# A rank scatter kernel: four groups in the Pool ring, twelve tiles as row copies, no drain flag, and a split last scatter

## The chip, the cores and the metric

The kernel runs on one core of one Trainium2 chip. The metric is device time in microseconds (us) of one execution; medians are of the runs of one kernel. The span of the profile is some 1.7 us shorter than the time, because it counts from the first to the last record of the core. Words used below: a *transfer* is one DMA that Pool issues, a load or a scatter; the *last landing* is the end of the last DMA packet; the *drain* is the instruction DRAIN of Pool near the end of a run, whose start and length are read from its record in the trace (no view of the profile lists it).

## The reference

```python
def reference(x, scores):          # x: 8 x 2048 x 2560 float32, scores: 8 x 2048
    order = np.argsort(scores, axis=1)
    ranks = np.argsort(order, axis=1)
    out = np.zeros_like(x)
    out[np.arange(8)[:, None], ranks, :] = x
    return out
```

Every row of 10 KB of `x` goes to the place in its batch that the rank of its score names: 168 MB read, 168 MB written, and no arithmetic on the rows.

## The kernel before

VectorE (DVE) counts the ranks. The rows move in two ways. A *bulk* tile is loaded into SBUF by GpSimd (Pool) as 128 partitions of two neighbouring rows (a group with two columns, 2560 KB) or one (a group with one column, 1280 KB), and written by one indirect scatter of 128 rows per column. A *row-copied* tile is written from DRAM to DRAM, one DMA of 10 KB for each row, issued by SP and Activation (ACT) in turn. The tiles of a group that are row-copied stand in the third place of `GROUPS`: all eight of the first column and three of the second, eleven tiles of 128 rows.

```python
GROUPS = [(0, 1, range(B)), (P, 1, range(3))] + [(256 * i, 2, ()) for i in range(1, 8)]
ORDER = [2, 0, 1, 3, 4, 5, 6, 7, 8]
SPLIT = ()          # groups whose scatters go out as the last 2 rows and the first 126
NBUF = 8            # SBUF buffers of the Pool ring
LAG = 2             # a load waits for the scatters of the group LAG places back
...
with tc.tile_critical(no_gpsimd_drain=True):
    ...
    # SP and ACT: 16 rows at a time, addresses read into registers
    for i in range(G):
        line.eng.dma_start(out=out_bytes[bass.ds(at[i], ROW)],
                           in_=x_bytes[b, row, :]).then_inc(s_rows[line], 16)
    ...
    for k in range(1, NBUF):
        load(pl, k, s_load[k])
    for k, (b, g) in enumerate(BULK):
        i = k % NBUF
        if k >= LAG and k + NBUF - LAG < len(BULK):
            scatters_done(pl, k - LAG)                  # Pool blocks here
            load(pl, k + NBUF - LAG, s_load[(k - LAG) % NBUF])
        ...                                             # wait for load k and its ranks
        for j in range(GROUPS[g][1]):
            scatter(k, j, 0, P, rank_i, s_scat[i][j])   # or the 2 and 126 rows of SPLIT
    for k in range(max(0, len(BULK) - NBUF), len(BULK)):
        scatters_done(sp, k)
```

## Time and profile before

| | before |
|---|---|
| time, median of 3 runs (lowest to highest) | 794.85 us (794.8 to 796.62) |
| span of the profiled execution | 795.4 us |
| DMA packets, bytes | 70737, 321.57 MB |
| last DMA packet ends | 790.9 us |
| Pool drain in the final barrier | 791.64 us, 3.0 us long |

The profile says that the sixteen DMA engines are busy nearly all the time, so the DMA engine that ends last is expected to set the time. Its main lines stand in the prediction below. Two more: how long a load takes from issue to landing (the issues of Pool: direction, engine, operation, count, size, median us), and SP's wait in the final barrier (total us, times, longest). The first says how much is queued ahead of a load; in the second SP waits 2.9 us after everything has landed, while Pool drains.

```profile
x<-in_x_dram POOLq DMA_DIRECT2D x55, 2560.0 KB, 19.2
out_dram<-x,rank_i POOLq DMA_INDIRECT x117, 23.5
```
```profile
SPq L420 <- PEq L420: 3.3, 2, 2.9
```

One caution belongs here. The profiled execution of before was a slowish one: it took 797.09 us.

### The profile page before, as it was taken

To read this page: it belongs to the slowest core of one execution; us is meant where nothing else is said; L and a number is where in the kernel's file an instruction comes from. 1 tells how busy PE (TensorE), PEld (TensorE's weight loads), DVE (VectorE), ACT (ScalarE), POOL (GpSimd) and SP (SyncE) were. 2 spreads that over 40 slices of the span, in tenths; PEclk is the share of its full clock that TensorE was granted. 3 is DMA by queue.
4 is the path that set the end of the run, shared out by engine and by line. 5 is a ranking of instruction groups with operands and counts; after the bars stand their busy time and mean duration, and the time that the engine had idled before them with its cause. 6 is when DMAs were issued, how large, how long until landed. Compare 5 with 4: busy or idle time off the path is not lost.

```text
span 795.4 us, 4586 instructions
## 1 busy us (share of the span) xinstructions
PE 33.3 (4%) x155; PEld 27.2 (3%) x155; DVE 411.2 (52%) x1002; POOL 148.4 (19%) x186
## 2 busy tenths in 40 slices
PE   3002010020020100200000000000000000000000
PEld 3001010010010100100000000000000000000000
DVE  6999999999999999999994000000000000000000
POOL 3102121212121212022111212122121212111600
PEclk9555555555555555555555555555555555555555
DMA  8999999999999999999999999999999999999994
GB/s 364 431 402 365 424 415 425 417 422 417 425 417 418 347 420 422 422 367 420 421 420 423 397 397 421 420 419 380 420 411 423 420 386 407 401 431 426 390 428 193
DMA packets 70737, 321.57 MB, mean 404 GB/s; under 512 B 25384, under 2 KB 47912, under 8 KB 47912
## 3 DMA queue, kind: packets, MB, share of 16 engines
q0 software_dynamic: 25488, 304.10, 91.3%
q1 hardware_dynamic: 22688, 9.94, 4.9%
q10 hardware_dynamic: 22528, 7.25, 3.9%
q14 instruction: 32, 0.26, 0.1%
q8 instruction: 1, 0.02, 0.0%
HBM read 167.84 MB, written 167.77 MB: 422 GB/s over the span
## 4 chain that ended last, share of the span: by engine, by line
DVE 47%; DMA 40%; issue 4%; POOL 3%; PE 1%; POOLq 0%; SPq 0%
DVE trash L258 41%; DMA out_dram<-x,rank_i 38%; DVE s_all L235 2%; DMA x<-in_x_dram 2%; POOL out_dram L361 2%; DVE rank L284 1%; DVE rank L290 1%; DVE rank_i L307 1%; POOL x L122 1%; DMA s_in<-in_scores_dram 0%; PE ps_all L190 0%; PE ps_col L169 0%; DVE rows_i L220 0%; POOLq L28 0%; DVE s_col L177 0%
## 5 line engine op out<-in xcount | busy, mean ns | idle before, releaser
L258 DVE TENSOR_SCALAR_CACHE_REDUCE trash<-s_all,s_col 128x1792 bf16<-128x1792 f32 (+9 forms) x248 | 315.3, 1306 | 0.3
L122 POOL DMA_DIRECT2D x<-in_x_dram x60 | 33.8, 565 | 545.8 <-DMA out_dram<-x,rank_i 376.5
L361 POOL DMA_INDIRECT out_dram<-x,rank_i x117 | 112.8, 964 | 59.0 <-issue 35.3
L258 DVE SCALAR_TENSOR_TENSOR trash<-s_all,s_col,mask 128x256 bf16<-128x256 f32 (+1 forms) x128 | 59.0, 461 | 0.0
L190 PE MATMUL ps_all<-ident,s_col 128*128 128x128 f32 x128 | 27.2, 399 | 247.4 <-DVE s_all L235 247.0
L190 PEld LDWEIGHTS ps_all<-ident,s_col 128*128 128x128 f32 x128 | 24.4, 213 | 249.4 <-DVE s_all L235 249.0
L235 DVE COPY s_all<-ps_all 128x512 f32<-128x512 f32 x32 | 20.1, 683 | 1.8 <-PE ps_all L190 1.5
L258 DVE DVE_READ_ACCUMULATOR trash<-s_all,s_col 128x1 f32 x248 | 19.9, 80 | 0.0
L290 DVE TENSOR_TENSOR rank<-rank,acc 128x2 f32<-128x2 f32 (+1 forms) x72 | 11.5, 160 | 2.5
L284 DVE TENSOR_TENSOR rank<-acc,acc 128x2 f32<-128x2 f32 (+1 forms) x72 | 11.5, 160 | 2.5
L307 DVE CAST rank_i<-rank 128x2 int32<-128x2 f32 (+1 forms) x61 | 10.7, 176 | 1.8
L258 DVE DVE_READ_ACCUMULATOR trash<-s_all,s_col,mask 128x1 f32 x128 | 10.2, 80 | 0.0
L300 PE MATMUL ps_row<-ident,rank 128*1 128x128 f32 x11 | 4.1, 372 | 101.3 <-DVE rank L290 92.7
L300 PEld LDWEIGHTS ps_row<-ident,rank 128*1 128x1 f32 x11 | 0.9, 79 | 105.0 <-DVE rank L290 95.5
L220 DVE TENSOR_SCALAR rows_i<-ps_row 1x128 int32<-1x128 f32 x11 | 3.0, 272 | 0.0
L177 DVE COPY s_col<-ps_col 128x128 f32<-128x128 f32 x1 | 0.3, 292 | 4.8 <-PE ps_col L169 4.8
L169 PE MATMUL ps_col<-ident,s_in 8*128 8x8 f32 x16 | 2.0, 261 | 4.0 <-DMA s_in<-in_scores_dram 4.0
L169 PEld LDWEIGHTS ps_col<-ident,s_in 8*128 8x128 f32 x16 | 1.9, 211 | 4.0 <-DMA s_in<-in_scores_dram 4.0
L150 POOL TENSOR_SCALAR_AFFINE_SELECT mask<-mask 128x256 f32<-128x256 f32 x2 | 0.8, 398 | 0.0
L162 DVE MEMSET acc<- 128x128 f32 x1 | 0.2, 165 | 1.1 <-SPq L98 1.1
L133 POOL MEMSET mask<- 128x512 f32 x1 | 0.5, 525 | 0.0
L132 POOL MEMSET ident<- 128x128 f32 x1 | 0.2, 204 | 0.5 <-SPq L98 0.5
(5 smaller groups left out, 0.7 us busy)
## 6 DMA issues: line engine op xcount, KB each, us to landing
x<-in_x_dram POOLq DMA_DIRECT2D x55, 2560.0 KB, 19.2
out_dram<-in_x_dram SPq DMA_DIRECT2D x704, 10.0 KB
out_dram<-in_x_dram ACTq DMA_DIRECT2D x704, 10.0 KB
x<-in_x_dram POOLq DMA_DIRECT2D x5, 1280.0 KB, 16.7
x<-in_x_dram SPq DMA_DIRECT2D x1, 2560.0 KB, 13.4
out_dram<-x,rank_i POOLq DMA_INDIRECT x117, 23.5
s_in<-in_scores_dram SPq DMA_DIRECT2D x1, 64.0 KB
```

What stands on the lines that cost most here:

```text
L122: line.eng.dma_start(out=xb[k % NBUF][:, :m * D], in_=x[b, r:r + P * m, :].rearrange("(p j) d -> p (j d)", j=m),).then_inc(sem, 16)
L150: nc.gpsimd.affine_select(out=part, in_=part, pattern=[[0, MMAX], [-1, P]], compare_op=OP.is_ge, fill=0.0, base=-half, channel_multiplier=1,)
L169: nc.tensor.transpose(out=ps_col[:, B * c:B * (c + 1)], in_=s_in[:, r + j:r + m * P:m], identity=ident[:B, :B],)
L190: nc.tensor.transpose(out=ps_all[:, P * c:P * (c + 1)], in_=s_col[:, c, b:b + 1].to_broadcast([P, P]), identity=ident[:],)
L220: nc.vector.tensor_scalar(out=rows_i[DIRECT.index((b, g))][:m, :], in0=ps_row[:m, :P], scalar1=float(b * N), scalar2=float(ROW), op0=OP.ad ...
L235: nc.vector.tensor_copy(out=s_all[:, 512 * q:512 * (q + 1)], in_=ps_all[:, 512 * q:512 * (q + 1)],)
L258: how.pop("do")(out=trash[i][:, :P * (hi_c - lo_c)], in0=s_all[:, P * lo_c:P * hi_c], accum_out=acc[which][:, col:col + 1], **how,)
L284: nc.vector.tensor_tensor(out=rank[:, cols], in0=acc[0][:, cols], in1=acc[1][:, cols], op=OP.add)
L290: nc.vector.tensor_tensor(out=rank[:, cols], in0=rank[:, cols], in1=acc[2][:, cols], op=OP.add)
L300: nc.tensor.transpose(out=ps_row[:m, :P], in_=rank[:, cols], identity=ident[:])
L307: nc.vector.tensor_copy(out=rank_i[:, cols], in_=rank[:, cols])
L361: nc.gpsimd.indirect_dma_start(out=out_flat, out_offset=bass.IndirectOffsetOnAxis(ap=index[:hi - lo, col:col + 1], axis=0), in_=xb[k % NBU ...
```

## The change

The intent: keep more groups queued, so that no DMA engine runs dry behind Pool's waits (LAG 2 to 4, no one-column groups, plain order); move one more tile from the bulk path to row copies (12 tiles: both columns of the first group, for six batches); let Pool drain before the closing block's last signals rather than in the final barrier; and split the last group's scatters in 2 and 126 rows, so that the sixteen engines end more evenly.

```diff
-    GROUPS = [(0, 1, range(B)), (P, 1, range(3))] + [(256 * i, 2, ()) for i in range(1, 8)]
-    ORDER = [2, 0, 1, 3, 4, 5, 6, 7, 8]
+    GROUPS = [(0, 2, range(6))] + [(256 * i, 2, ()) for i in range(1, 8)]
+    ORDER = range(8)
...
-    SPLIT = ()
+    SPLIT = [(7, 7)]
     LAST = 2
     NBUF = 8
-    LAG = 2
+    LAG = 4
...
-    with tc.tile_critical(no_gpsimd_drain=True):
+    with tc.tile_critical():
```

## The prediction

> **What bounds the kernel now.** I read the page's queue and busy rows first, then a table of windows, then Pool's waits and its timeline, and last the raw records behind them: each DMA packet's start and length, and the sixteen completion increments of each DMA.
>
> The page's busy row of the 16 DMA engines, and its queues (packets, MB, share of 16 engines):
>
> ```profile
> DMA  8999999999999999999999999999999999999994
> ...
> q0 software_dynamic: 25488, 304.10, 91.3%
> q1 hardware_dynamic: 22688, 9.94, 4.9%
> q10 hardware_dynamic: 22528, 7.25, 3.9%
> ```
>
> The shares add to 100.1%: the DMA engines are the bound. DVE ends at about 426 us and Pool is 19% busy; DVE is named on the first half of the chain of waits only because it happened to run beside Pool's waits. q0 carries loads and scatters, q1 and q10 the 1408 row copies.
>
> Full is not the same as useful. Windows of the same profile (PE, PEld, DVE, POOL busy, clock, DMA share, GB/s):
>
> ```profile
> 60.00:70.00 10.00, 3.67 (x16) 3.27 (x16) 9.79 (x22) 2.50 (x3) 0.64 1.07 359
> 260.00:270.00 10.00, 0.00 (x0) 0.00 (x0) 9.76 (x26) 2.49 (x3) 0.50 1.08 311
> 740.00:750.00 10.00, 0.00 (x0) 0.00 (x0) 0.00 (x0) 7.20 (x8) 0.50 0.99 381
> 760.00:770.00 10.00, 0.00 (x0) 0.00 (x0) 0.00 (x0) 0.00 (x0) 0.50 1.01 429
> ...
> 784.00:786.00 2.00, 0.00 (x0) 0.00 (x0) 0.00 (x0) 0.00 (x0) 0.50 0.14 56
> 786.00:788.00 2.00, 0.00 (x0) 0.00 (x0) 0.00 (x0) 0.00 (x0) 0.50 0.06 26
> ```
>
> 429 is full speed; 311 to 381 at a share near 1 means packets that wait inside (first packets of a load took 1.2 to 2.2 us in the records instead of 0.76). From 784 us the share is 0.06, one engine of sixteen: **a single DMA engine works on alone until 791**. The increments say the same of the whole run: in the last scatter 15 engines land within 1.1 us and one 6.1 us later, and from about 160 us on one lags by 5 to 9 us in nearly every transfer. I call it the slow engine. I could not read its number.
>
> Pool's waits (total us, times, longest), then one line of its timeline:
>
> ```profile
> POOL x L122 <- DMA out_dram<-x,rank_i: 376.5, 37, 31.5
> ```
> ```profile
> 63.73 0.57 POOL L122 DMA_DIRECT2D x<-in_x_dram  x1 [31.46 <-DMA out_dram<-x,rank_i]
> ```
>
> Before each load Pool waits for all sixteen increments of the scatters two groups back, that is for the slow engine. The others then hold one load and one group of scatters, about 12.5 us of work, less their lead of up to 9 us and about 4 us until a new load reaches them. Behind a one-column group it is half of that. So they run dry (263 to 272, 340, 440 to 480, 540, 640 to 690, 735 to 745 us); at each such place the lag shrinks by 1 to 5 us. The 63.73 line is the worst case: only the first two groups' scatters had been issued before Pool blocked, and just one was left when it woke.
>
> **What the Trainium skill says.** "DMA: Bandwidth & Descriptors", section "Queues, rings and completion order": an engine round-robins between its queue rows by packet. The trace agrees: on the slow engine row copies and q0 packets, completion packets included, go one to one (44 to 44 from 280 to 300 us). Same page, "Why a DMA increments its semaphore by 16 and not by 1": only the full 16 means landed, and the number of engines is the largest divisor up to 16 of the slowest dimension, with an exception for some GpSimd copies that puts ceil(n/16) partitions on each. So 126 rows would be 9 on each of 14 engines, or 8 on fifteen and 6 on the last; no run here shows which. Same page, "Latency and other measured facts": engines 7 and 15 are usually slower. The trace shows one slow engine, in phases with loads only (the lag grows from 7.0 to 8.8 us between 700 and 745 us, and stays at 7.2 in the scatters after 751).
>
> **The change, part by part.** What counts is the slow engine, which ends at 791 us; 4.4 us of ending follow it.
>
> Its account now, worked out from packet lengths in the records (0.381 us per 10 KB of q0, 0.757 per 20 KB, 0.034 for a row copy's share of 640 bytes with its completion): 440 x 0.757 + 976 x 0.381 + 1408 x 0.034 = 753, its 8 packets of the first load 6, some instruction fetches and the scores about 2, so 761. It starts at 2.1 us and its first packets are 2.3 us long: 765. 791 - 765 = 26 us are left to explain. Between the dry places its lag grows by some 2.6% of the time (4.7 to 8.9 us from 113 to 272; 4.5 to 7.1 from 360 to 440), over 735 us about 19: its own slowness, which nothing in the change removes. The remainder, some 7, is what it loses itself at the dry places. A second reading: the last increments of consecutive transfers are 6.2 to 6.8 us apart for a load, but 10.4 after the 63.73 line (69.9 to 80.3), 8.2 at 280, and 0.4 to 1 too long at six later places: 3.8 + 1.5 + 3.6 = 9. I take 8.
>
> - Four groups in the ring, and no one-column groups. Scatters of four groups go out before the first wait (their ranks are ready by an estimated 42 us, while eight loads fill the queue to 56), and in steady state three groups, 37 us, stay queued behind the one waited for. That is more than any lead I expect (19 plus a few). All dry places go. The 15 fast engines gain some 17 us, but this is not in the sum: they only wait longer at the end. For the slow engine: **-8**.
> - Twelve tiles. Per engine a bulk tile is 16 x 0.381 = 6.1 us, a row-copied one 128 x 0.034 = 4.4: **-1.7**. DVE changes by a 2048-wide pass for a 1920-wide and a 128-wide one; it is idle after 426 us anyway.
> - Order 0, 1, 2...: the first scatter's ranks come one group, about 6 us, later, behind queued loads: 0.
> - Row copies reaching the end: 1536 rows against 57 x 9 + 116 x 9 = 1557 q0 packets, some 20 of them before the first row. At one to one they last as long as q0 itself, where before they ended at 727 on the slow engine. I estimate 10 to 20 rows left over; alone in the dry places, rows took 0.3 us each, several beside each other: **+2**.
> - Split scatters: if the slow engine is one of two left out by 14 engines of 9 rows, it loses 14 packets, -5.3; if it is the last of ceil(126/16), 4 packets, -1.5; else 0 to +0.8. My mixture: **-1.5**. The two added issues (1.25 us) lie far ahead of the data.
> - Pool drain. In the trace a GpSimd drain of 3.0 us starts at 791.64, in the final barrier. With the flag gone a drain takes the place of a NOP that waits for the same signal of SP at 791.56. I expect the 3 us to move forward by 0.1 and SP's collecting to come after it: **+0.2**, not -3.
>
> Sum: -8 - 1.7 + 2 - 1.5 + 0.2 = -9, so 794.85 becomes **786**.
>
> **The rivals.** *All the fast engines' gain counts*: if the slowness moves from engine to engine with the dry places, a loose ring averages it, the time falls by 17 or more to about 775. For it: after 272 us several engines lag 6 to 7.5 us. Against: the same growth returns after every reset. *Nothing to gain*: if the slow engine never waits and merely looks slow at the dry places, only 1.7 us and the split remain: 791 to 795. For it: at 340 to 357 us its transfers are evenly spaced although the others ran dry. *The row copies become the end*: the slots are used up, and the SP and Activation queues run on after q0, 5 to 10 us; 792 to 798. For it is the count 1536 to 1537; against it that 10 KB packets at the end give rows twice as many turns per us as 20 KB loads. *A really early drain* (beginning when Pool has issued its last, hidden beside the transfers) would take 3 us off each of these.
>
> **Range and chances.** The sum's uncertain terms are the 8 (4 to 13), the split (-5 to +1), the rows (0 to 8) and the drain (-3 to +0.3); together some 6 us either way. Low 777: first rival in part, or a lucky split and an early drain. High 795: second or third rival. 2% faster is 779, at the low edge, which needs two lucky terms: 0.17. 2% slower is 811, which needs a new stall: 0.02.
>
> **What would show it.** Right: window rates of 410 to 425 GB/s with no dip between 60 and 75 us or later; fifteen engines done some 15 to 20 us before the end and a share of 0.06 for that long; Pool's load waits all on scatters four groups back, no rates below 380 before 745; row copies issued until about 750; the drain 3 us long after the last landing. Wrong: an even end (all engines within 3 us) would say that the slowness was made by the ring; dips that stay would say it was not the depth; a last landing on q1 or q10 would be the third rival; a tail of one engine below 10 us with an unchanged time would say the lag was a sum I misread.

## The result

| | before | after |
|---|---|---|
| time, median of 4 runs | 794.83 us | 801.3 us (801.17 to 801.36) |
| ratio | | 1.0076, 95% interval 1.0059 to 1.0094 |
| span of the profiled execution | 795.4 us | 799.6 us |
| DMA packets, bytes | 70737, 321.57 MB | 74355, 320.29 MB |
| last q0 packet, last row copy end | 790.9, 726.8 us | 790.9, 790.9 us |
| Pool drain: start, length | 791.64, 3.0 us | 791.78, 7.0 us |

A ratio here and below is the mean time of one kernel's fast runs over that of the other's of the same rounds, so it is not quite the ratio of the medians quoted beside it. The change made the kernel slower by 6.5 us, outside the predicted range of 777 to 795 us.

The page's busy row of the DMA engines and its queues, after:

```profile
DMA  8999999999999999999999999999999999999930
...
q0 software_dynamic: 25008, 301.48, 88.8%
q1 hardware_dynamic: 24736, 10.60, 4.9%
q10 hardware_dynamic: 24576, 7.91, 4.0%
```

The last two slices now read 3 and 0 where before only the last was short, with a 4: the engines as a group end earlier. q0 (Pool's transfers) carries 480 packets fewer and q1 and q10 (the row copies) 4096 more, which goes with a twelfth row-copied tile, 32 packets for each of its 128 rows.

Windows after (columns as in the prediction: PE, PEld, DVE, POOL busy, clock, DMA share, GB/s):

```profile
60.00:70.00 10.00, 3.72 (x17) 3.29 (x17) 9.89 (x15) 2.49 (x3) 0.67 1.02 413
260.00:270.00 10.00, 0.20 (x1) 0.20 (x2) 9.72 (x27) 2.48 (x3) 0.50 1.04 431
740.00:750.00 10.00, 0.00 (x0) 0.00 (x0) 0.00 (x0) 1.90 (x2) 0.50 1.03 417
750.00:760.00 10.00, 0.00 (x0) 0.00 (x0) 0.00 (x0) 3.69 (x4) 0.50 0.96 359
760.00:770.00 10.00, 0.00 (x0) 0.00 (x0) 0.00 (x0) 0.00 (x0) 0.50 0.65 229
770.00:780.00 10.00, 0.00 (x0) 0.00 (x0) 0.00 (x0) 0.00 (x0) 0.50 0.08 28
780.00:790.00 10.00, 0.00 (x0) 0.00 (x0) 0.00 (x0) 0.00 (x0) 0.50 0.06 25
```

The three places that moved 359, 311 and 381 GB/s before now move 413, 431 and 417: these dips are gone, and from 60 to 750 us no window of 10 us is below 410. Two low ones are left: 374 GB/s from 50 to 60 us (381 before), and a new one of 359 from 750 to 760 us, where Pool waits for the last load before it issues the last scatters. From 770 us on the share is 0.06 to 0.08, one engine of sixteen. It works alone for some 20 us (from 771), where it had 6 before, and it ends at the same 790.9.

Pool's waits for its loads, the line of its timeline that answers to the one in the prediction, and its issues:

```profile
POOL x L122 <- DMA out_dram<-x,rank_i: 343.7, 33, 19.0
```
```profile
63.23 0.57 POOL L122 DMA_DIRECT2D x<-in_x_dram  x1 [18.99 <-DMA out_dram<-x,rank_i]
```
```profile
x<-in_x_dram POOLq DMA_DIRECT2D x57, 2560.0 KB, 46.5
...
out_dram<-x,rank_i POOLq DMA_INDIRECT x116, 51.1
```

The first wait fell from 31.5 to 19.0 us because four groups of scatters go out ahead of it. A load now lands 46.5 us after its issue instead of 19.2: that much is queued ahead. Pool still waits for 344 us, but from 60 to 750 us the rates show no sign that the DMA engines run dry behind it.

SP's wait at the end, after:

```profile
SPq L98 <- POOLq L98: 6.8, 1, 6.8
```

SP now waits on Pool at line 98, the closing of the block, as the missing flag makes it, and 6.8 us instead of 2.9.

**Where the 6.5 us come from.** Spans of typical executions, before (from b1, the kernel before without the flag, so with the same DMA program) against after: last landing 788.7 and 790.9 (+2.2); from there to the start of Pool's drain 0.6 and 0.9 (+0.3); the drain 3.0 and 7.0 (+4.0); the rest 0.8 and 0.8. The sum is +6.5, against spans of 793.2 and 799.6 (+6.4); the +2.2 is little more than what equal programs differ by (below), the +4.0 is clear. So there are two questions: why did the transfers not end 8 us earlier, and why is the drain longer?

### The profile page after: what moved, and what is told of

It is laid out like the page before. It is cut to its first block, busy times and chain, and to the rows that moved or that the text cites. A ratio compares the mean times of both kernels' runs of the same rounds, so it can differ in the third digit from the quotient of the medians.

```text
span 799.6 us, 4803 instructions
## 1 busy us (share of the span) xinstructions
PE 33.3 (4%) x152; PEld 28.7 (4%) x152; DVE 409.0 (51%) x963; POOL 147.6 (18%) x184
## 2 busy tenths in 40 slices
DMA packets 74355, 320.29 MB, mean 401 GB/s; under 512 B 27464, under 2 KB 52040, under 8 KB 52040
## 4 chain that ended last, share of the span: by engine, by line
DVE 45%; another core or an unknown queue 31%; POOL 8%; DMA 6%; issue 4%; PE 1%; POOLq 0%; SPq 0%
DVE trash L258 39%; POOL out_dram L361 6%; DMA x<-in_x_dram 6%; DVE s_all L235 2%; POOL x L122 2%; DVE rank L284 1%; DVE rank L290 1%; DVE rank_i L307 1%; PE ps_all L190 0%; DMA s_in<-in_scores_dram 0%; PE ps_col L169 0%; DVE rows_i L220 0%; POOLq L28 0%; DVE s_col L177 0%
## 5 line engine op out<-in xcount | busy, mean ns | idle before, releaser
L258 DVE TENSOR_SCALAR_CACHE_REDUCE trash<-s_all,s_col 128x1792 bf16<-128x1792 f32 (+7 forms) x240 | 314.4, 1344 | 0.3
L122 POOL DMA_DIRECT2D x<-in_x_dram x57 | 32.1, 563 | 510.4 <-DMA out_dram<-x,rank_i 343.7
L258 DVE SCALAR_TENSOR_TENSOR trash<-s_all,s_col,mask 128x256 bf16<-128x256 f32 x128 | 61.3, 479 | 0.0
L190 PE MATMUL ps_all<-ident,s_col 128*128 128x128 f32 x128 | 29.1, 421 | 275.1 <-DVE s_all L235 274.7
L190 PEld LDWEIGHTS ps_all<-ident,s_col 128*128 128x128 f32 x128 | 26.1, 227 | 277.0 <-DVE s_all L235 276.6
L290 DVE TENSOR_TENSOR rank<-rank,acc 128x2 f32<-128x2 f32 x64 | 10.3, 162 | 2.2
L284 DVE TENSOR_TENSOR rank<-acc,acc 128x2 f32<-128x2 f32 x64 | 10.3, 161 | 2.2
L307 DVE CAST rank_i<-rank 128x2 int32<-128x2 f32 x58 | 9.9, 171 | 1.8
L361 POOL DMA_INDIRECT out_dram<-x,rank_t x2 | 1.7, 872 | 11.6 <-DMA x<-in_x_dram 11.3
L300 PE MATMUL ps_row<-ident,rank 128*2 128x128 f32 x6 | 1.9, 322 | 13.3 <-DVE rank L290 13.3
L300 PEld LDWEIGHTS ps_row<-ident,rank 128*2 128x2 f32 x6 | 0.5, 80 | 15.6 <-DVE rank L290 15.6
## 6 DMA issues: line engine op xcount, KB each, us to landing
x<-in_x_dram POOLq DMA_DIRECT2D x57, 2560.0 KB, 46.5
```

The source lines that it names most:

```text
L122: line.eng.dma_start(out=xb[k % NBUF][:, :m * D], in_=x[b, r:r + P * m, :].rearrange("(p j) d -> p (j d)", j=m),).then_inc(sem, 16)
L190: nc.tensor.transpose(out=ps_all[:, P * c:P * (c + 1)], in_=s_col[:, c, b:b + 1].to_broadcast([P, P]), identity=ident[:],)
L258: how.pop("do")(out=trash[i][:, :P * (hi_c - lo_c)], in0=s_all[:, P * lo_c:P * hi_c], accum_out=acc[which][:, col:col + 1], **how,)
L284: nc.vector.tensor_tensor(out=rank[:, cols], in0=acc[0][:, cols], in1=acc[1][:, cols], op=OP.add)
L290: nc.vector.tensor_tensor(out=rank[:, cols], in0=rank[:, cols], in1=acc[2][:, cols], op=OP.add)
L300: nc.tensor.transpose(out=ps_row[:m, :P], in_=rank[:, cols], identity=ident[:])
```

## The experiments

My theory after the result: one DMA engine is slow by itself and has its own sum of work, so the ring gives it nothing; the split puts 9 packets on it and costs time; the drain is longer for a reason to be found. Rivals: the ring does help and something else takes the gain away (the split, the row copies at the end); the drain is long because of the missing flag, or because row copies are still in flight, or because of the number of Pool's transfers. Eighteen kernels were run, all with correct results, each against runs of the kernel before on the same chip (median 794.75 to 795.63 us). Last landings of kernels with the same DMA program differ by about 1 to 2 us (790.9 and 788.7; 790.9 and 789.7), so a landing alone settles nothing below that.

| run | time, us | ratio (95%) | last landing | Pool drain, us | Pool transfers |
|---|---|---|---|---|---|
| a1_flag_back | 800.23 | 1.0070 (1.0056-1.0083) | 789.7 | 7.010 | 175 |
| a2_two_groups | 801.14 | 1.0077 (1.0064-1.0091) | 791.6 | 7.010 | 175 |
| a3_no_split | 798.88 | 1.0051 (1.0037-1.0064) | 788.0 | 6.847 | 173 |
| b1_drain_alone | 795.12 | 1.0007 (0.9993-1.0020) | 788.7 | 3.011 | 177 |
| b2_four_groups | 793.69 | 0.9985 (0.9971-0.9999) | 787.4 | 3.178 | 177 |
| b3_twelve_tiles | 798.50 | 1.0047 (1.0034-1.0061) | 787.2 | 6.847 | 173 |
| c1_126_first | 802.80 | 1.0100 (1.0085-1.0116) | 791.7 | 7.010 | 175 |
| d1_ten_tiles | 797.48 | 1.0032 (1.0020-1.0045) | 787.2 | 7.092 | 176 |
| b4_split_alone | 799.61 | 1.0053 (1.0039-1.0067) | 793.4 | 3.178 | 179 |
| e1_rows_ten | 794.37 | 0.9986 (0.9972-1.0000) | 788.0 | 3.178 | 177 |
| e2_rows_five | 794.39 | 0.9985 (0.9972-0.9999) | 788.0 | 3.178 | 177 |
| e3_two_splits | 804.99 | 1.0118 (1.0103-1.0133) | 794.7 | 7.173 | 177 |
| g1_early_drain | 792.08 | 0.9956 (0.9936-0.9976) | 787.4 | 32.0, early | 177 |
| g2_extra_7_8_15 | 808.62 | 1.0161 (1.0138-1.0184) | 802.5 | 3.178 | 177 |
| g3_extra_4_10_12 | 803.52 | 1.0098 (1.0078-1.0118) | 797.4 | 3.178 | 177 |
| g4_one_column_kept | 799.70 | 1.0051 (1.0030-1.0071) | 787.9 | 8.725 | 175 |
| h1_low_engines | 818.15 | 1.0293 (1.0277-1.0309) | 813.5 | 32.1, early | 176 |
| h2_changed_early_drain | 796.54 | 1.0018 (1.0005-1.0032) | 789.9 | 40.1, early | 175 |

### Undoing one part of the change

**a1_flag_back**: the flag is put back.

```diff
-    with tc.tile_critical():
+    with tc.tile_critical(no_gpsimd_drain=True):
```

> The changed kernel with the Pool drain taken out of the end of the section again. Theory A (the drain is the whole loss): the last landing stays at 791 us, the drain in the final barrier is 3.0 us again, and the time falls from 801.3 to about 795 to 796, that is level with the kernel before within 0.3%. Rival B (the loss is in the transfers, or the longer drain belongs to the new scatters): the drain in the final barrier is 7 us and the time stays above 799.

800.23 us, with the drain back in the final barrier and as long as in the changed kernel, 7.010 us. The flag decides where the drain stands and not how long it is.

**a2_two_groups**: the ring of the changed kernel goes back to two groups.

```diff
-    LAG = 4
+    LAG = 2
```

> The changed kernel with two groups in the ring in place of four. Theory A (one DMA engine's own slowness sets the end; the ring only lets the others run ahead): the dips in GB/s and the resets of the lag come back, the slow engine's last landing stays within 1.5 us of 791, and the time is 800 to 803. Rival B (my prediction's step: the dry places cost the slow engine 8 us, and something else in the change took them back): the last landing moves to 797 or later and the time to 807 or more.

801.14 us, the same as the changed kernel. Its windows:

```profile
60.00:70.00 10.00, 4.05 (x17) 3.35 (x17) 9.89 (x15) 2.49 (x3) 0.50 1.09 362
...
770.00:780.00 10.00, 0.00 (x0) 0.00 (x0) 0.00 (x0) 0.00 (x0) 0.50 0.78 293
780.00:790.00 10.00, 0.00 (x0) 0.00 (x0) 0.00 (x0) 0.00 (x0) 0.50 0.13 39
```

The early dip is back (362 GB/s), and the fifteen fast engines work on until about 778 us, where most had ended by 767. The end has not moved. Ten microseconds of fifteen engines are worth nothing here.

**a3_no_split**: no split.

```diff
-    SPLIT = [(7, 7)]
+    SPLIT = ()
```

> The changed kernel with the last group scattered whole. The trace of the changed kernel shows 9 packets of 10 KB for the slow engine in each 126-row scatter, so Theory A (14 engines of 9 rows, the slow one among them): the last landing 0.8 to 1.2 us earlier, the time 800.2 to 800.6, the drain still near 7 us. Rival B (the split itself makes the drain long, as its scatters use 2 and 14 engines): the drain is back at 3 us and the time near 796.

798.88 us, so the split costs the changed kernel 2.4 us. Row copies end 0.2 us after the last scatter in this run, and 1.7 us pass from there to the drain instead of 0.9. Taking this part out leaves 4 us still lost.

**c1_126_first**: the 126 rows are issued ahead of the 2.

```diff
-                    scatter(k, j, P - LAST, P, rank_t, s_last[i][j])
                     scatter(k, j, 0, P - LAST, rank_i, s_scat[i][j])
+                    scatter(k, j, P - LAST, P, rank_t, s_last[i][j])
```

> The changed kernel with the 126-row scatter ahead of the 2-row one. If the engines for 126 rows are 14 consecutive ones from a cursor that stands at the first engine, they are now the first 14, and the 2 rows go to the last two. Theory A (the slow engine is one of the last two): it has 1 packet in place of 9 in each of the two scatters, 16 fewer at 0.415 us, so the last landing comes 6.6 us earlier, near 784, and the time is 794 to 795. Rival B (the slow engine is another, or there is no such cursor): within 1 us of the changed kernel, 800 to 802.

802.8 us: no relief. The packet records show 9 packets of 10 KB on the slow engine, alone by then, for each scatter of 126 rows, as in the changed kernel, where each holds it for some 3.8 us (783.1 to 787.0 and 787.2 to 790.9). If 126 rows go to 14 engines of 9 rows, the slow engine was not one of the two left out in either order.

**d1_ten_tiles**: ten tiles instead of twelve, and no split, so that the row copies end long before q0.

```diff
-    GROUPS = [(0, 2, range(6))] + ...
+    GROUPS = [(0, 2, range(5))] + ...
-    SPLIT = [(7, 7)]
+    SPLIT = ()
```

> The changed kernel without the split and with 10 tiles of row copies in place of 12, so that the row copies end well before the last scatters on the slow engine. Theory A (row copies run beside the drain's queue to the end and that is why the drain is long): the drain is near 3 us. Rival B (the drain counts Pool's own transfers, 176 here against 173 without the split): the drain stays at 6.8 to 7.1 us. By packet lengths two more bulk tiles cost the slow engine 3.4 us, so the last landing at 790 to 793.

797.48 us; the last row copy ends at 672 us and the drain still takes 7.092. So row copies near the end are not why it is long. The last landing is 787.2, against 788.0 of a3 with two tiles more and 787.4 to 788.0 of b2, e1 and e2 with one more: by packet lengths two tiles more in bulk should have cost 3.4 us. A row-copied tile is worth nothing that these runs can resolve.

### One part of the change alone

**b1_drain_alone**: the kernel before, without the flag.

```diff
-    with tc.tile_critical(no_gpsimd_drain=True):
+    with tc.tile_critical():
```

> The kernel before with the drain at the end of the section as the only edit. Theory A (where the drain stands decides its length): 7 us of drain after the last landing at 791, time 800 to 801. Rival B (the length comes from other parts of the change): a drain of 3 us and a time of 795 to 796.

795.12 against 794.9 us: +0.2, within the noise (interval 0.9993 to 1.0020), with a drain of 3.011 us that starts 0.6 us after the last landing.

**b2_four_groups**: the kernel before with four groups in the ring.

```diff
-    LAG = 2
+    LAG = 4
```

> The kernel before with four groups in the ring as the only edit. Theory A (the slow engine's own work sets the end, the ring gives nothing): the others end near 770 and the slow engine at 788 to 792, the drain is 3.0 us, time 794 to 796. Rival B (the ring does give the slow engine something when the row copies are not also made more): last landing at 783 or earlier, time below 789.

793.69 against 794.91 us, a gain of 1.2. Its windows:

```profile
60.00:70.00 10.00, 3.67 (x16) 3.27 (x16) 9.83 (x21) 2.50 (x3) 0.50 1.03 417
...
760.00:770.00 10.00, 0.00 (x0) 0.00 (x0) 0.00 (x0) 0.00 (x0) 0.50 0.63 262
770.00:780.00 10.00, 0.00 (x0) 0.00 (x0) 0.00 (x0) 0.00 (x0) 0.50 0.07 29
780.00:790.00 10.00, 0.00 (x0) 0.00 (x0) 0.00 (x0) 0.00 (x0) 0.50 0.05 19
```

Before, 359 GB/s from 60 to 70 us; here 417. Before, one engine was alone from about 785 us on; here from about 771 (most of the others end by 766). The ring does to the kernel before just what was predicted of it, and the end moves by 1.2 us. This is the plainest of the eighteen runs: the ring's effect on the fast engines and its lack of effect on the time, with nothing else changed.

**b3_twelve_tiles**: the kernel before with the new groups and order, eleven row-copied tiles becoming twelve and no one-column groups.

```diff
-    GROUPS = [(0, 1, range(B)), (P, 1, range(3))] + [(256 * i, 2, ()) for i in range(1, 8)]
-    ORDER = [2, 0, 1, 3, 4, 5, 6, 7, 8]
+    GROUPS = [(0, 2, range(6))] + [(256 * i, 2, ()) for i in range(1, 8)]
+    ORDER = range(8)
```

> The kernel before with the new groups and their order (12 tiles of row copies, no one-column groups) as the only edit: two groups in the ring, no split, no drain in the section. Theory A (the longer drain comes with this part, the only one not yet tried alone): the drain is 6.8 us as in the changed kernel without the split, last landing at 788 to 791, time 798 to 800. Rival B (the long drain needs two parts together): drain 3 us, time 793 to 796.

798.5 us, +3.6. The last landing is 787.2, no later than before, 1.8 us pass from there to the drain instead of 0.6, and SP waits for Pool's drain in the final barrier:

```profile
SPq L420 <- PEq L420: 7.1, 2, 6.7
```

The line names PE, which comes last in the barrier's chain; the drain's own record says 6.847 us. This part of the change brings the long drain, with two groups in the ring and with the flag in place.

**b4_split_alone**: the kernel before with the split (its last group is number 8).

```diff
-    SPLIT = ()
+    SPLIT = [(7, 8)]
```

> The kernel before with the last group's scatters split as the only edit (179 transfers of Pool in place of 177). Theory A (126 rows go as 9 to each of 14 engines, the slow one among them): the slow engine has 2 packets of 10 KB more, 0.8 us, time 795.3 to 796.5; the drain grows by 0.16 us if each transfer still open costs 0.08, as between 173, 175 and 176 in the runs so far. Rival B (the split helps where no row copies run beside it): last landing earlier than the kernel before's 788.7 to 790.9, time below 794.

799.61 us, +4.0, and the last landing moves to 793.4, with a drain of only 3.178. That is more than one added packet of 0.38 us for each of two scatters can make. Windows of this run, then of the kernel before:

```profile
775.00:780.00 5.00, 0.00 (x0) 0.00 (x0) 0.00 (x0) 0.00 (x0) 0.50 1.01 401
780.00:785.00 5.00, 0.00 (x0) 0.00 (x0) 0.00 (x0) 0.00 (x0) 0.50 0.89 309
785.00:790.00 5.00, 0.00 (x0) 0.00 (x0) 0.00 (x0) 0.00 (x0) 0.50 0.19 74
```
```profile
775.00:780.00 5.00, 0.00 (x0) 0.00 (x0) 0.00 (x0) 0.00 (x0) 0.50 1.01 430
780.00:785.00 5.00, 0.00 (x0) 0.00 (x0) 0.00 (x0) 0.00 (x0) 0.50 0.82 348
```

From 775 to 780 us the share is the same, 1.01, and the rate falls from 430 to 401 GB/s: packets wait inside. In the records of 770 to 795 us 37 of 603 packets of 10 KB took over 500 ns (17.6 us beyond 385 ns each, over all engines), and none of 606 in the kernel before. So the split costs more than its packet count. Slow packets aren't peculiar to it, though: from 755 to 770 us a3, without a split, has 26 of 343 over 500 ns, the changed kernel 51 of 339, and b2 none of 453. Why packets are slower was not tested, nor how many of the slow ones lie on the slow engine.

**e3_two_splits**: the changed kernel with the last two groups split.

```diff
-    SPLIT = [(7, 7)]
+    SPLIT = [(7, 6), (7, 7)]
```

> The changed kernel with the last two groups split, for the drain: 177 transfers of Pool in place of 175. Theory A (the drain works through what Pool's ring has not yet retired, and a fixed number of transfers brings a retirement: 177 gave 3.0 to 3.2 us in the kernel before, 173 to 176 gave 6.8 to 7.1): the drain is 3 to 3.5 us, time near 799. Rival B (the groups' shapes decide, not the count): 7.17 us, time 802 to 803.

804.99 us, 3.7 more than the changed kernel with one split. The drain takes 7.173 us at 177 Pool transfers, the same number as the kernel before, with 3.0 us: the number of transfers is not what makes it long.

### Is it one engine with its own sum of work?

**g2_extra_7_8_15** and **g3_extra_4_10_12**: b2 with six short extra copies at the start, on SP's queue. The Trainium skill, "DMA: Bandwidth & Descriptors", section "Why a DMA increments its semaphore by 16 and not by 1", says that a DMA issued by SP with k pieces uses the lowest-numbered k engines. So copies with 7, 8 and 15 pieces of 60 KB (2.27 us each in the records), two of each, load engines 0 to 6 with 13.7 us, 7 with 9.1, 8 to 14 with 4.6 and 15 with nothing; 4, 10 and 12 pieces load 0 to 3 with 13.7, 4 to 9 with 9.1, 10 and 11 with 4.6 and the rest with nothing. If one engine's own sum sets the end, the end moves by that engine's extra.

```diff
+        EXTRA = (7, 8, 15) * 2          # g3: (4, 10, 12) * 2
+        scratch = nc.dram_tensor("scratch", (6, 16, 7 * D), F32, kind="Internal").ap()
...
+        for i, n in enumerate(EXTRA):
+            sp.eng.dma_start(
+                out=scratch[i, :n, :6 * D],
+                in_=x[i, :7 * n, :].rearrange("(p j) d -> p (j d)", j=7)[:, :6 * D],
+            ).then_inc(s_extra, 16)
...
+        sp.wait(s_extra, 16 * len(EXTRA))
```

> The kernel before with four groups in the ring (793.7 to 794.4 us), plus at the start two copies of 60 KB on each of the lowest 7, two on the lowest 8 and two on the lowest 15 engines, 2.3 us each: 13.7 us more work for engines 0 to 6, 9.1 for 7, 4.6 for 8 to 14, none for 15. Theory A (the end is one engine's own work): the end moves by that engine's share, so 794 (it is 15), 798.7 (8 to 14), 803.2 (7) or 807.8 (0 to 6). Rival B (work is shared, the end isn't one engine's): the mean of the added work over sixteen engines, 8.6 us, so 802.7, or all hidden behind other waits. The next run keeps 802.7 and 803.2 apart.

> The same with 4, 10 and 12 in place of 7, 8 and 15: 13.7 us more for engines 0 to 3, 9.1 for 4 to 9, 4.6 for 10 and 11, none for 12 to 15; the mean is 7.4. Theory A: the end moves to 807.8, 803.2, 798.7 or 794; with the other run: engine 7 gives 803.2 in both, engine 15 gives 794 in both. Rival B: 801.5.

808.62 and 803.52 us: 14.5 and 9.4 more than b2's 794.1 (its 793.69 scaled from its own chip's 794.91 to this one's 795.29). If all engines shared the extra, it would be the mean, 8.6 and 7.4. The last 10 us of each:

```profile
790.00:800.00 10.00, 0.00 (x0) 0.00 (x0) 0.00 (x0) 0.00 (x0) 0.50 0.06 27
```
```profile
790.00:800.00 10.00, 0.00 (x0) 0.00 (x0) 0.00 (x0) 0.00 (x0) 0.50 0.05 19
```

In both one engine is still at it alone when the others have been done for long. 14.5 fits the 13.7 of engines 0 to 6, 9.4 the 9.1 of engines 4 to 9; both hold for engines 4, 5 and 6 alone. No record names an engine, so the numbers rest on the rule of the skill, but the records bear out how many engines were loaded. In g2, where the others run dry for a moment, packets of over 5 KB keep 8.1 engines busy from 761 to 762 us and 7.1 from 770 to 772; in g3 10.1 from 766 to 767, and 5.0 from 776 to 778, which is four and the slow one. By that rule the slow engine of this chip is one of those three, and what is put on it at the start comes back at the end, within 1 us.

**h1_low_engines**: g1 (below) with one whole load issued by SP in pieces of 124 and 4 partitions, which the same rule puts on engines 0 to 3, to take that load away from the slow engine.

```diff
+        for lo, hi in ((0, 124), (124, P)):
+            sp.eng.dma_start(out=xb[LOW][lo:hi, :m * D],
+                             in_=tile_rows[lo:hi, :]).then_inc(s_low, 16)
```

> The kernel with four groups in the ring and the early explicit drain (792.1 us), with one of the 59 full loads issued by SP as 124 and 4 partitions, which should put all of it on engines 0 to 3: each of these gets 32 packets of 0.757 us in place of 8, +18 us, where they have 22 us of lead; every other engine loses 6.1 us. Theory A (the end is the work of one engine of 4 to 6): the last landing moves from 787.4 to 781 to 783 and the time to 786 to 788. Rival B (the slow engine only looks slow because it is last in some shared order, and another takes its place when it is relieved): less than 2 us, 790 to 792.

818.15 us, a miss of its own design. The load went out at the start, where engines 0 to 3 had no lead to spend:

```profile
50.00:60.00 10.00, 0.00 (x0) 0.00 (x0) 9.83 (x27) 1.90 (x2) 0.50 1.02 243
90.00:100.00 10.00, 0.00 (x0) 0.00 (x0) 9.79 (x28) 0.00 (x0) 0.50 0.51 189
```

Four engines shared themselves between it and q0 until about 87 us (the four late increments of each transfer), Pool's first wait, for the scatters of the first group, ended at 106 us, and the other twelve ran out of work (a share of 0.51 from 90 to 100 us). At the end five engines are still busy from 794 to 805 us and four until 809, which fits engines 0 to 3 as the last ones. Whether relief of the slow engine shortens the kernel is therefore still only argued, from the opposite experiment, g2 and g3.

**e1_rows_ten** and **e2_rows_five**: b2, with 6 of 16 row copies given as 10 pieces of 1 KB (4 of 16 as 5 pieces of 2 KB), meant, by the rule cited for g2, to run on the ten (five) lowest-numbered engines alone and so to take row copies off the upper ones.

```diff
+                dst, src = out_bytes[bass.ds(at[i], ROW)], x_bytes[b, row, :]
+                if i % 3 == 0:                              # e2: i % 5 == 0, a=5
+                    dst = dst.rearrange("(a e) -> a e", a=10)
+                    src = src.rearrange("(a e) -> a e", a=10)
+                line.eng.dma_start(out=dst, in_=src).then_inc(s_rows[line], 16)
```

> The kernel before with four groups in the ring, and 6 of 16 row copies cut into 10 pieces of 1 KB[...]. 528 such rows: an engine among the ten takes 0.044 us in place of 0.034 for each, +5 us; the other six lose 0.034 each, -18 us. Theory A (the end is the slow engine's own work) with the slow engine among the last six: it ends near 770 and the lower ten, at 765 to 772, are level with it: time 775 to 781. With the slow engine among the ten: +5 us, time 798 to 800. Rival B (the end isn't any one engine's work): 793 to 795 as without the edit.

> As the other, but 4 of 16 row copies cut into 5 pieces of 2 KB[...]. 352 such rows: the five take 0.082 us in place of 0.034, +17 us, which uses up the lead they have; the other eleven lose 12 us. Slow engine among the eleven: its end near 776, time 782 to 786. Slow engine among the five: time 808 to 812. Together with the other run this places it in 0 to 4, 5 to 9 or 10 to 15.

Both failed as experiments: the packet counts are those of b2, so the contiguous row was cut in 16 pieces of 640 bytes all the same. They serve as two repeats of b2 on another chip: ratios of 0.9986 and 0.9985 to before, where b2 had 0.9985.

### The drain

**g4_one_column_kept**: b2 with twelve row-copied tiles but four one-column groups kept.

```diff
-    GROUPS = [(0, 1, range(B)), (P, 1, range(3))] + ...
+    GROUPS = [(0, 1, range(B)), (P, 1, range(4))] + ...
```

> The kernel before with four groups in the ring and 12 tiles of row copies, four one-column groups kept (175 transfers of Pool). Theory A (the one-column groups keep the drain short): the drain is 3.0 to 3.2 us, time 792.5 to 794.5. Rival B (twelve tiles make it long): 7 us, time 797 to 799.

799.7 us, all of it the drain: 8.725 us, the longest of all, after a last landing of 787.9. So it is not the absence of one-column groups that makes the drain long.

Call kernels a family that take their groups from the same side of the change: the changed kernel, a1, a2, a3, b3, c1, d1 and e3 in one; the kernel before, b1, b2, b4, e1, e2, g2 and g3 in the other. In the changed family the length follows the number of Pool's transfers, to the nanosecond, whatever the flag and the ring do (7.010 in the changed kernel, a1, a2 and c1), and grows by 0.08 us per transfer: 6.847, 7.010, 7.092 and 7.173 us for 173, 175, 176 and 177. In the family of before the ring does count a little: at 177 transfers 3.011 and 3.015 us with two groups, 3.178 with four. Between families it jumps (3.0 us at 177 transfers before, 8.7 at 175 in g4). What decides the jump is open: not the flag, the ring alone, row copies near the end, the number of transfers or the one-column groups.

One regularity in the table narrows it. Divided by 0.0815 us, (7.173 - 6.847) / 4, every drain that starts after the last landing is a whole number to within 0.1: 37 and 39 in the family of before, 84, 86, 87 and 88 in the changed one, 107 in g4. As an estimate, then, the drain takes 0.0815 us for each of the last so many transfers: in the changed family for all behind the 89th, before for those behind the 140th (138th with four groups), in g4 behind the 68th. The jump would lie in how many earlier transfers were already done with; why it is that many is not shown.

**g1_early_drain**: b2 with an explicit drain of Pool right after its last scatter is issued.

```diff
+
+        nc.gpsimd.drain()
```

> The kernel before with four groups in the ring, and an explicit Pool drain directly behind Pool's last scatter. That kernel takes 793.7 to 794.4 us with a drain of 3.2 us after the last landing. Theory A (the drain works through Pool's unretired transfers at 0.08 us each, and can do so while the others are still on their way): the explicit drain ends within 0.3 us of the last landing, the one in the final barrier is below 0.3 us, time 790.5 to 791.5. Rival B (its time begins only after the last landing): 3 us still follow, time 793.5 to 794.5.

792.08 against 795.29 us, 0.9956: the best version of all, 2.0 us below b2 (794.1, scaled to this chip). The drain begins at 757.3 and ends at 789.3, 1.9 us after the last landing at 787.4, where the plain drain would take 3.2. SP's wait for it:

```profile
SPq L98 <- POOLq L98: 1.2, 1, 1.2
```

**h2_changed_early_drain**: the changed kernel with the same line.

> The changed kernel with an explicit Pool drain directly behind Pool's last scatter. Its drain of 7.0 us starts at 791.8, after the last landing. Theory A (work on unretired transfers, mostly hidden when it starts at 759): 1.5 to 2 us follow the last landing in place of 7, time 795.5 to 797. Rival B (it comes after the last landing whatever its start): 800.5 to 801.5.

796.54 us, 4.8 less than the changed kernel, which is slower than before by 0.2% only. The drain runs from 753.7 to 793.8 us, and 3.9 of its 7 us still follow the last landing at 789.9:

```profile
SPq L98 <- POOLq L98: 3.0, 1, 3.0
```

In these two runs about half of the drain lay beside the transfers; the rest seems to need the last landing. This was not tested further.

## Why the prediction was wrong

The prediction had the bound right (one DMA engine that ends alone) and the mechanism of the ring right; it failed in the size of its terms, three of them above all: the ring, the drain and the split.

- **Ring, "-8": wrong, and the main step that failed.** It said of the slow engine's unexplained time that "the remainder, some 7, is what it loses itself at the dry places", averaged that with a second reading of 9, and took 8. The runs show about 1 (b2, e1, e2: ratios 0.9985 and 0.9986) or nothing (a2 against the changed kernel). By the same account the changed kernel's slow engine has 456 x 0.757 + 930 x 0.381 + 8 x 0.757 + 1536 x 0.034 = 758, with the 2 of fetches and scores and the 4.4 of the start 764; it ends at 790.9, so some 27 us stay unexplained with no dry place left, against 26 in the kernel before. So the unexplained time does not come from the dry places and stays with that engine. Its lag (the last increment of a transfer less the first) grows all along, 2.2 us at 56, 9.3 at 270, 15.6 at 437, 20.4 at 586 us: 3.2 to 3.8% of the time between these points where nothing runs dry, instead of the 2.6% read before. Only the first of the prediction's two stretches gives 2.6%; the second, 4.5 to 7.1 us from 360 to 440, gives 3.3%, which over 735 us is 24 us and leaves 2 of the 26, not 7. A lag behind engines that themselves stand still now and then comes out too small, and a remainder from it need not be a loss. The gaps that the second reading counted were there, but closing them gave the slow engine about 1 us and not 9; what it did in them was not read from its packets. The rival "nothing to gain" named this.
- **Fast engines, 17 us not in the sum: right.** Most end by 767 us, the last of the fifteen at 771, and they only wait longer.
- **Pool drain, "+0.2": its place right, its size wrong.** It moved forward and SP waits for it at line 98, as predicted; b1 measures +0.2 for this part alone. But it was taken to stay at 3.0 us, from the trace of before. It is 7.0, +4.0, and b3 shows that it comes with the new groups (6.847 us there). This is the larger half of the 6.5 us, and no rival had it.
- **Split, "-1.5": wrong in its sign.** Of the three cases in the mixture, it is 9 rows each on 14 engines with the slow one among them, the case given "0 to +0.8". Measured are +2.4 (a3 against the changed kernel) and +4.0 (b4 alone). The two added packets are 0.8 of it and the drain, for two more transfers, 0.16; the rest may be slower packets, which is not shown for the slow engine.
- **Twelfth tile, "-1.7": not seen.** With four groups in the ring, ten, eleven and twelve tiles land at 787.2, 787.4 to 788.0, and 788.0; with two, b3 lands 1.5 us before b1. All are inside the scatter of equal programs. If the first three are taken at their word, a row copy costs the slow engine as much as its share of a bulk row, 6.1 / 128 = 0.048 us, and not the 0.034 of the sum: an estimate, untested.
- **Row copies at the end, "+2": about 0.** At one to one nothing is left over: the last row copy ends at 790.904 us and the last q0 packet at 790.909. What it costs is the ending, 0.9 instead of 0.6 us from landing to drain (1.7 and 1.8 in a3 and b3, where rows end 0.2 us after q0). The third rival is true to that extent.
- **The early drain rival**: it does not come from the flag. It comes from an explicit drain, at about half of what was hoped (g1, h2).

Put together, the parts alone on the kernel before: +0.2 (flag), -1.2 (ring), +3.6 (groups and tiles, the drain in it), +4.0 (split). The sum is +6.6, measured +6.5; as the split alone costs more than within the changed kernel and the ring less there, the agreement is partly luck.

What stays open: why one DMA engine is 3% slower than the others (b2 on chip 10, e1 on 1, g1 on 2 and h2 on 0 all end on one engine alone, from 772 to about 787 us or later, so it is not a fault of one chip), whether taking work off it shortens the kernel, why some packets at the end are slower, and what sets the drain's length between families.

## What to carry to other kernels

When one of sixteen DMA engines ends last, write down that engine's own packets and start the sum there: freeing the other fifteen only lengthens their wait, and a lag read against engines that stand still now and then is too small. A probe that puts known extra work on chosen engines told here within two runs that one engine sets the end, and nearly which. Check the length of Pool's drain whenever its groups of transfers change, and if it shows at the end, try to issue it right after the last transfer: here that hid about half of it.

## What the Trainium skill lacked or had wrong

- "DMA: Bandwidth & Descriptors", section "Latency and other measured facts": engines 7 and 15 are given as the usually slower ones. Here one engine ends some 20 us after the rest, and on the chip of g2 and g3 the 14.5 and 9.4 us added to the end put it among 4, 5 and 6, by the page's own rule for which engines a DMA uses.
- The same page, "Why a DMA increments its semaphore by 16 and not by 1": its rule for the number of engines fits an indirect scatter of 126 rows, with 9 packets on the slow engine in the changed kernel (14 engines of 9), not the ceil(n/16) of the exception, which would be at most 8. What it lacks is that packets can get slower around such scatters: 37 of 603 over 500 ns in b4, none of 606 before (but also 26 of 343 in a3, without a split).
- No page that I found has the cost of Pool's drain at the end of a kernel: 3.0 to 8.7 us here, 0.0815 us for each of 37 to 107 transfers (an estimate), about half of it hidden when it is issued early in g1 and h2.
